# A two-layer decoder on one core: shift and scale sums by transposes with VectorE's part two blocks later, constants among the first weight blocks, and the up-projection's relu and square on ScalarE

## The chip, the cores and the metric

The kernel runs on one core of a Trainium2 chip. The metric is the time of one execution on the device in microseconds (us); a median over several runs is given. Five engines work side by side, each in the order of its own queue: PE (TensorE, matrix products into PSUM, with PEld its weight loads), DVE (VectorE), ACT (ScalarE), POOL (GpSimd) and SP (SyncE, which here issues all the DMA transfers). An engine waits only where an instruction needs something that another engine or a transfer has not delivered.

## The reference, cut to what matters

Two decoder layers on 256 rows of 2048 columns. Each layer takes six vectors of 2048 from one condition vector c (shift, scale and gate, for attention and for the MLP), and uses shift and scale to turn x into the input h of a projection.

```python
c_act = jax.nn.silu(c)
for l in range(DEPTH):
    mod = c_act @ w_ada[l] + b_ada[l]                 # w_ada[l]: 2048 x 12288
    sh_a, sc_a, g_a, sh_m, sc_m, g_m = jnp.split(mod[:, None, :], 6, axis=-1)
    h = x * (1.0 + sc_a) + sh_a
    y = _mixer(h, ...)                                # input projection, attention, output projection
    x = _layernorm(ALPHA * x + (1.0 + g_a) * y, ln1_g[l], ln1_b[l])
    h = x * (1.0 + sc_m) + sh_m
    y = jnp.square(jax.nn.relu(h @ w_up[l])) @ w_down[l]
    x = _layernorm(ALPHA * x + (1.0 + g_m) * y, ln2_g[l], ln2_b[l])
```

All is float32. Each product is formed from a high and a low part in a shorter format (`hi*hi + hi*lo + lo*hi`), so a weight block is split once, and every output needs three products.

## The kernel before, in words

**Blocks.** Weights come in blocks of 128 partitions x 1024 numbers (512 KB). A block is loaded into `raw` by SP (L139; 7 buffers), copied into a high part `wh` by ACT (L133), and DVE subtracts to get the low part `wl` (L134; 3 buffers each for `wh` and `wl`). PE then runs the products of the block (L290 to L292, L316 to L319, or L897 and L899 in the up-projection). The function `block` counts blocks; between blocks it does other pieces of work that are queued in lists.

**The condition vectors.** They stream through the same `raw` buffers (`rawa`, L155 and L183) among the weight blocks, at a rate per block (`side_rate`). In `ada_T` DVE multiplies 16 such blocks by one number per partition each and adds them up in `acc` (L145 for the first, L147 for the other 15; `acc` has one buffer). That leaves 128 partitions x 2 x 512 partial sums, which have to be added over the partitions and laid out with the column number on the partition. `finish` does it: PE multiplies each 128 columns of `acc` by a column of ones (L163, eight products of one column each, which the profile shows as 16 instructions), into one PSUM bank, and DVE adds the bias (L167, two instructions) to get four columns of two vectors in `modT`. There are 16 such finishes, four for each pair of vectors. A finish is put into `pending`, and `settle` runs it at the next block or when its result is wanted. The gate vectors go through `ada_G`, with a finish of their own.

**The start.** Layer 0's input projection runs in four passes over a quarter of the depth each (`first_pass`), since h of a quarter needs the shift and scale of that quarter only. Before the first pass come 16 blocks `rawa`, a finish, and `make_h`: PE transposes x (L460), ACT applies scale and shift (L473), DVE splits h into `hT` (L475, L476). The constants (masks, the tables sin and cos, the transposed norm parameters, lambda) are set up by `constants()` between those 16 blocks. Before each later pass, again, a finish and a `make_h` have to be through.

**The up-projection.** Four PSUM tiles are filled per 512 columns. In `up_out` ACT copies one half of each out (L914), DVE adds the other half (L915) and forms max(t,0)*t (L916), ACT copies the high part of the result into `Hs` (L923), DVE subtracts for the low part (L924). For the first eight sets of layer 0, which run in two halves (`part` is given), ACT forms relu and square instead (L919, L920).

**The order.** Each engine's instructions are put in order when the program is built, by a scheduler that goes by priorities (the order of the code) and by estimated durations; tiles wait for a free buffer of their pool. PSUM has four buffers for products (`mm`) and four for all else (`bank`).

## Time and profile before

| | before |
|---|---|
| time, median of 3 runs | 2384.29 us (2381.55 to 2387.99) |
| the profiled execution: its time | 2385.05 us |
| the profiled execution: its span | 2383.3 us |
| busy PE / DVE / ACT | 2300.8 / 1798.7 / 1106.1 us |
| DMA, mean rate | 260 GB/s |

The span is what the trace covers; the execution took 1.75 us more. Busy time is the sum over an engine's instructions without overlap. PE's busy time contains whatever its pipeline leaves between two products, so it is read by the starts of successive instructions as well. In a row of the list of instructions the first number is the start, the second the time, and a bracket says how long the engine was idle before it and what ended that.

### The profile page before, as it was taken

The numbers are of one execution on the slowest core, as the hardware profiler recorded it, in microseconds if no ns is written. First come the engines' busy times: TensorE is split into PE (matmuls) and PEld (weight loads), VectorE is DVE, ScalarE is ACT, GpSimd is POOL, SyncE is SP. The second block draws the span as 40 slices with busy tenths as digits, with TensorE's granted clock in tenths as the row PEclk, the third lists the DMA queues.
The fourth block names the chain that finished last, engine by engine and source line by source line (L and its number), as shares of the span: only waits on it lengthen the run. The fifth ranks groups of instructions, "written<-read, shape, count | busy, mean of one in ns | idle before, by whom it ended". The sixth has DMA issues, their size and how long they took to land.

```text
span 2383.3 us, 33425 instructions
## 1 busy us (share of the span) xinstructions
PE 2300.8 (97%) x12572; PEld 1977.8 (83%) x12572; DVE 1798.7 (75%) x2355; ACT 1106.1 (46%) x1589; POOL 36.9 (2%) x60
## 2 busy tenths in 40 slices
PE   4999999899999999999999999999999999999998
PEld 3887798799989788888877778977888888888886
DVE  7788988878888678879877876667685666665667
ACT  3543675344546344344444564544444443543442
POOL 0000010000000000000000000000000000000000
PEclk9999999999999999999999999999999999999999
DMA  9999688888998888888858977764687777756653
GB/s 313 341 321 314 203 265 302 315 295 308 321 326 306 281 284 307 303 281 301 290 175 290 311 225 242 234 214 168 218 267 247 230 236 247 230 191 192 187 190 124
DMA packets 309891, 619.39 MB, mean 260 GB/s; under 512 B 24200, under 2 KB 25048, under 8 KB 309728
## 3 DMA queue, kind: packets, MB, share of 16 engines
q1 hardware_dynamic: 309728, 617.25, 77.0%
q8 instruction: 98, 1.61, 0.3%
q14 instruction: 65, 0.53, 0.1%
HBM read 615.07 MB, written 2.10 MB: 259 GB/s over the span
## 4 chain that ended last, share of the span: by engine, by line
PE 81%; DVE 8%; DMA 6%; issue 3%; ACT 2%; POOL 0%; DVEq 0%; SPq 0%; ACTq 0%; POOLq 0%
PE mm L291 13%; PE mm L292 13%; PE mm L290 13%; PE mm L897 7%; PE bank L897 7%; PE mm L319 5%; PE mm L318 5%; PE mm L316 5%; DMA rawa<-in_w_ada_dram 5%; PE mm L899 4%; PE bank L899 4%; DVE wl L134 3%; DVE acc L147 2%; PE bank L163 1%; DMA raw<-in_w_in_dram 1%
## 5 line engine op out<-in xcount | busy, mean ns | idle before, releaser
L133 ACT CAST wh<-raw 128x1024 fp32r<-128x1024 f32 x752 | 788.9, 1052 | 958.5 <-PE mm L292 493.0
L134 DVE TENSOR_TENSOR wl<-raw,wh 128x1024 fp32r<-128x1024 f32 x752 | 913.5, 1221 | 345.6 <-ACT wh L133 341.8
L147 DVE SCALAR_TENSOR_TENSOR acc<-rawa,cact,acc 128x1024 f32<-128x1024 f32 x368 | 471.1, 1280 | 138.4 <-DMA rawa<-in_w_ada_dram 136.7
L291 PE MATMUL mm<-wl,Hs 128*128 128x512 f32 x992 | 386.7, 390 | 3.2 <-DVE wl L134 3.2
L290 PE MATMUL mm<-wh,Hs 128*128 128x512 f32 x992 | 386.2, 389 | 0.0
L292 PE MATMUL mm<-wh,Hs 128*128 128x512 f32 x992 | 386.1, 389 | 0.0
L319 PE MATMUL mm<-hT,wl 128*128 128x256 f32 x1024 | 289.4, 285 | 4.8 <-DVE wl L134 4.8
L316 PE MATMUL mm<-hT,wh 128*128 128x256 f32 x1024 | 291.1, 286 | 1.5 <-DVE hT L475 1.1
L318 PE MATMUL mm<-hT,wh 128*128 128x256 f32 x1024 | 290.3, 284 | 0.8 <-DVE hT L476 0.8
L897 PE MATMUL mm<-hT,wh 128*128 128x512 f32 x768 | 288.0, 398 | 0.1
L897 PE MATMUL bank<-hT,wh 128*128 128x512 f32 x768 | 287.0, 396 | 0.0
L291 PEld LDWEIGHTS mm<-wl,Hs 128*128 128x128 f32 x992 | 186.2, 188 | 43.8 <-DVE wl L134 5.3
L290 PEld LDWEIGHTS mm<-wh,Hs 128*128 128x128 f32 x992 | 186.2, 188 | 38.8
L292 PEld LDWEIGHTS mm<-wh,Hs 128*128 128x128 f32 x992 | 186.2, 188 | 38.4
L899 PE MATMUL mm<-hT,wl 128*128 128x256 f32 x768 | 215.6, 281 | 1.0 <-DVE wl L134 1.0
L899 PE MATMUL bank<-hT,wl 128*128 128x256 f32 x768 | 215.2, 280 | 0.0
L291 PE MATMUL mm<-wl,hT 128*128 128x512 f32 x512 | 202.6, 396 | 2.0 <-DVE wl L134 1.8
L290 PE MATMUL mm<-wh,hT 128*128 128x512 f32 x512 | 199.8, 400 | 3.0 <-DVE hT L475 3.0
L319 PEld LDWEIGHTS mm<-hT,wl 128*128 128x128 f32 x1024 | 196.6, 193 | 6.4 <-DVE wl L134 6.2
L292 PE MATMUL mm<-wh,hT 128*128 128x512 f32 x512 | 200.8, 393 | 0.6 <-DVE hT L476 0.6
L316 PEld LDWEIGHTS mm<-hT,wh 128*128 128x128 f32 x1024 | 197.5, 193 | 3.1 <-DVE hT L475 1.4
L318 PEld LDWEIGHTS mm<-hT,wh 128*128 128x128 f32 x1024 | 197.6, 193 | 1.5 <-DVE hT L476 1.3
(249 smaller groups left out, 2653.7 us busy)
## 6 DMA issues: line engine op xcount, KB each, us to landing
rawa<-in_w_ada_dram SPq DMA_DIRECT2D x384, 512.0 KB, 5.3
raw<-in_w_up_dram SPq DMA_DIRECT2D x256, 512.0 KB, 4.6
raw<-in_w_down_dram SPq DMA_DIRECT2D x256, 512.0 KB, 5.2
raw<-in_w_in_dram SPq DMA_DIRECT2D x192, 512.0 KB, 5.4
raw<-in_w_o_dram SPq DMA_DIRECT2D x64, 512.0 KB, 5.3
gb<-in_ln_g_dram SPq DMA_DIRECT2D x12, 256.0 KB, 6.2
bb<-in_ln_b_dram SPq DMA_DIRECT2D x12, 256.0 KB, 6.9
xacc<-in_x_dram SPq DMA_DIRECT2D x8, 256.0 KB, 6.5
```

Source lines behind the costliest of these rows:

```text
L133: nc.scalar.copy(wh, raw)
L134: nc.vector.tensor_sub(wl, raw, wh.bitcast(F32))
L147: nc.vector.scalar_tensor_tensor(acc, raw, k, acc, ALU.mult, ALU.add)
L163: nc.tensor.matmul(ps[:, f:f + 1], lhsT=acc[:, f // 4, (f % 4) * P:(f % 4 + 1) * P], rhs=ones[:, 0:1], start=True, stop=True)
L290: nc.tensor.matmul(o, lhsT=hi, rhs=wh, start=start, stop=False)
L291: nc.tensor.matmul(o, lhsT=hi, rhs=wl, start=False, stop=False)
L292: nc.tensor.matmul(o, lhsT=lo, rhs=wh, start=False, stop=stop)
L316: nc.tensor.matmul(o, lhsT=wh[:, j, cs], rhs=hT[:, kt, 0, :], start=first and kt == kt0 and f % 2 == 0, stop=False)
L318: nc.tensor.matmul(o, lhsT=wh[:, j, cs], rhs=hT[:, kt, 1, :], start=False, stop=False)
L319: nc.tensor.matmul(o, lhsT=wl[:, j, cs], rhs=hT[:, kt, 0, :], start=False, stop=last and kt == kt1 - 1 and f % 2 == 1)
L897: nc.tensor.matmul(pu[f], lhsT=wh[:, j, cs], rhs=hT[:, kt].rearrange("p a s -> p (a s)"), start=kt == kt0, stop=False)
L899: nc.tensor.matmul(pu[f][:, 0:S], lhsT=wl[:, j, cs], rhs=hT[:, kt, 0, :], start=False, stop=kt == kt1 - 1)
```

## The change

The diff does three things. (1) The finish of a shift and scale sum: eight transposes of 128x128 into two PSUM banks in place of eight products with a column of ones, then, on DVE, one sum over the free axis for each bank (`reduce_sum`) and the addition of the bias. `finish` is now a generator: its PE part runs as before, its DVE part two blocks later (`LATER`), unless the result is wanted before. The four finishes of the first passes and whatever else is asked for by key run through at once. A gate's finish keeps its parts together and counts as ready two blocks later. (2) The start: the loads of three `rawa` blocks come ahead of x, the masks on POOL and the bias come next, and the rest of the constants is handed out one piece per block inside the first pass. (3) In `up_out` relu and square are two ACT instructions for all sets, where DVE had one.

```diff
+LATER = 2
@@
-    ones = const.tile([P, P], F32, name="ones")
-    nc.vector.memset(ones, 1.0)
+    one = const.tile([P, 1], F32, name="one")
+    nc.vector.memset(one, 1.0)
     ones_r = const.tile([P, P], F32R, name="ones_r")
-    nc.vector.tensor_copy(ones_r, ones)
+    nc.vector.memset(ones_r.bitcast(F32), 1.0)
@@
         def finish():
-            ps = bank()
-            for f in range(8):
-                nc.tensor.matmul(ps[:, f:f + 1], lhsT=acc[:, f // 4, (f % 4) * P:(f % 4 + 1) * P],
-                                 rhs=ones[:, 0:1], start=True, stop=True)
+            pss = []
             for i in range(2):
+                ps = bank()
+                for f in range(4):
+                    nc.tensor.transpose(ps[:, f * P:(f + 1) * P], acc[:, i, f * P:(f + 1) * P], ident)
+                pss.append(ps)
+            yield
+            for i, ps in enumerate(pss):
+                red = sm.tile([P, 4], F32, tag="red", name="red")
+                nc.vector.reduce_sum(red, ps.rearrange("p (f k) -> p f k", f=4), axis=mybir.AxisListType.X)
                 s0 = (vec + i) * KT + kt0
-                nc.vector.scalar_tensor_tensor(modT[l, vec + i][:, kt0:kt0 + 4], ps[:, 4 * i:4 * i + 4], float(i),
+                nc.vector.scalar_tensor_tensor(modT[l, vec + i][:, kt0:kt0 + 4], red, float(i),
                                                badaT[l][:, s0:s0 + 4], ALU.add, ALU.add)
 
-        pending[(l, vec, kt0)] = finish
+        pending[(l, vec, kt0)] = [0, finish()]
@@
     def settle(*keys):
-        for k in keys or list(pending):
-            if k in pending:
-                pending.pop(k)()
-                ready.add(k)
+        for k in list(keys or pending):
+            while k in pending and (keys or pending[k][0] <= count[0]):
+                if next(pending[k][1], keys) is keys:
+                    del pending[k]
+                    ready.add(k)
+                elif not keys:
+                    pending[k][0] = count[0] + LATER
+                    break
@@
-                    nc.vector.scalar_tensor_tensor(t2, t2, 0.0, t2, ALU.max, ALU.mult)
                 else:
                     nc.vector.tensor_add(t2, pu[f2 // 2], part[:, f2:f2 + 2, :])
-                    nc.scalar.activation(t2, t2, AF.Relu)
-                    nc.scalar.activation(t2, t2, AF.Square)
+                nc.scalar.activation(t2, t2, AF.Relu)
+                nc.scalar.activation(t2, t2, AF.Square)
@@
         if i == 0:
-            side.extend([x_rows(a, b)] + want_mod(0, 0, [a]))
-            side_pop()
+            side.extend(want_mod(0, 0, [a]))
+            for _ in range(3):
+                side_pop()
+            for _ in x_rows(a, b):
+                pass
+            bias_T(0)
+            masks()
             for k2 in range(a, b, 2):
                 turned[k2] = turn(k2)
-            for _ in constants():
-                side_pop()
         side_flush()
@@
+        if i == 0:
+            rest = constants()
+            for _ in range(12):
+                later.append(lambda: next(rest, None))
```

**Order at the start.** SP's issues from the first instruction of the program on, before (`crow` is c, `xacc` x, `r_...` and the small names are constants):

```order
L101 DMA crow<-in_c_dram 16x128
L1005 DMA xacc<-in_x_dram 128x512 x2
L384 DMA pos_i<-in_positions_dram 128x2x1
L119 DMA r_153<-in_b_ada_dram 96x128
L155 DMA rawa<-in_w_ada_dram 128x2x512
L419 DMA r_193<-in_ln_g_dram 32x128
L155 DMA rawa<-in_w_ada_dram 128x2x512
L419 DMA r_193<-in_ln_b_dram 32x128
L155 DMA rawa<-in_w_ada_dram 128x2x512
```

and in the changed program (the same queue, the same place):

```order
L102 DMA crow<-in_c_dram 16x128
L156 DMA rawa<-in_w_ada_dram 128x2x512 x3
L1015 DMA xacc<-in_x_dram 128x512 x2
L120 DMA r_119<-in_b_ada_dram 96x128
L156 DMA rawa<-in_w_ada_dram 128x2x512 x13
L140 DMA raw<-in_w_in_dram 128x2x512
```

The first `rawa` moves ahead of four other issues, and eleven small transfers are gone from among the 16. On ACT, before, the first instructions after the program's entry are these (the table for Sin, then sin of the angles, then the table for Silu and `cact`, by which all `rawa` are multiplied):

```order
L412 ACT_TABLE_LOAD
L412 ACTIVATE sinT<-ang 128x16
L107 ACT_TABLE_LOAD
L107 ACTIVATE cact<-bank 128x16
L413 ACTIVATE cosT<-ang 128x16
```

and in the changed program:

```order
L108 ACT_TABLE_LOAD
L108 ACTIVATE cact<-bank 128x16
L1019 ACTIVATE xacc<-xacc 128x512 x2
L134 CAST wh<-raw 128x1024 x2
L484 ACTIVATE h_222<-bank,mod_0_105,mod_1_106 128x256 x2
```

`cact` no longer stands behind the sine.

**Order at the first layer norm.** DVE's instructions at the change from attention to MLP in layer 0, before (`mv`, `ve`, `rs` are a row's statistics, L501 normalizes, L167 is the finish):

```order
L494 TENSOR_SCALAR ve<-mv 128x1
L488 BN_STATS stats<-xacc 128x6
L501 TENSOR_SCALAR xacc<-xacc,mv,rs 128x512 x4
L492 BN_AGGR mv<-stats 128x2
L167 SCALAR_TENSOR_TENSOR mod_3_1877<-bank,badaT_157 128x4
L494 TENSOR_SCALAR ve<-mv 128x1
L167 SCALAR_TENSOR_TENSOR mod_4_1878<-bank,badaT_157 128x4
L134 TENSOR_TENSOR wl<-raw,wh 128x1024
L501 TENSOR_SCALAR xacc<-xacc,mv,rs 128x512 x2
```

and in the changed program:

```order
L503 BN_AGGR mv<-stats 128x2
L148 SCALAR_TENSOR_TENSOR acc<-rawa,cact,acc 128x1024
L505 TENSOR_SCALAR ve<-mv 128x1
L503 BN_AGGR mv<-stats 128x2
L135 TENSOR_TENSOR wl<-raw,wh 128x1024
L512 TENSOR_SCALAR xacc<-xacc,mv,rs 128x512 x4
L505 TENSOR_SCALAR ve<-mv 128x1
L135 TENSOR_TENSOR wl<-raw,wh 128x1024
L512 TENSOR_SCALAR xacc<-xacc,mv,rs 128x512 x2
L171 TENSOR_REDUCE red<-bank 128x4 x2
```

The finish's DVE part stands behind the second row's statistics and its normalization; an accumulation (L148) has moved in ahead of the first row's.

**Order after a set of the up-projection.** ACT's instructions at the end of one full set, before:

```order
L914 COPY t_8769<-mm 128x256 x2
L914 COPY t_8777<-bank 128x256
L133 CAST wh<-raw 128x1024
L914 COPY t_8777<-bank 128x256
L923 CAST Hs<-t_8769 128x2x256
L133 CAST wh<-raw 128x1024
L923 CAST Hs<-t_8777 128x2x256
L133 CAST wh<-raw 128x1024 x6
```

and in the changed program:

```order
L925 COPY t_8821<-mm 128x256 x2
L925 COPY t_8830<-bank 128x256
L134 CAST wh<-raw 128x1024
L925 COPY t_8830<-bank 128x256
L929 ACTIVATE t_8821<-t_8821 128x512
L930 ACTIVATE t_8821<-t_8821 128x512
L929 ACTIVATE t_8830<-t_8830 128x512
L933 CAST Hs<-t_8821 128x2x256
L930 ACTIVATE t_8830<-t_8830 128x512
L134 CAST wh<-raw 128x1024
L933 CAST Hs<-t_8830 128x2x256
L134 CAST wh<-raw 128x1024 x6
```

Between the first and the second copy of a weight block there now stand five instructions where there were two. On PE the order of the weight products outside attention is nearly the same in both programs; where L163 stood eight times, L166 (the transpose) stands eight times. In the first passes the transposes of x have moved: ahead of the third pass all eight stand directly before the first product that needs them, where six had stood 34 products earlier.

## Rows read from the trace of the kernel before

**Rows 1.** The page's first part: busy time and share of each engine.
```profile
PE 2300.8 (97%) x12572; PEld 1977.8 (83%) x12572; DVE 1798.7 (75%) x2355; ACT 1106.1 (46%) x1589; POOL 36.9 (2%) x60
```
**Rows 2.** Stretches of 60 us: busy time of each engine, granted clock, DMA share, GB/s.
```profile
0.00:60.00 60.00, 27.95 (x110) 22.76 (x111) 42.32 (x73) 18.72 (x27) 4.08 (x28) 1.00 0.91 313
60.00:120.00 60.00, 58.64 (x359) 52.00 (x359) 47.22 (x46) 31.93 (x41) 0.00 (x0) 1.00 0.96 342
720.00:780.00 60.00, 60.00 (x444) 57.31 (x443) 50.79 (x51) 36.42 (x48) 0.00 (x0) 1.00 0.87 295
2340.00:2384.00 44.00, 32.19 (x143) 26.31 (x141) 30.66 (x42) 8.87 (x9) 1.83 (x2) 0.90 0.27 97
```
**Rows 3.** PE's waits over the span: total us, times, longest.
```profile
PE bank L121 <- DVE dots L436: 11.6, 1, 11.6
...
PE mm L291 <- DVE wl L134: 6.4, 9, 1.4
```
**Rows 4.** List of instructions, the start: start us, us, engine, line.
```profile
2.63 0.26 PE L105 MATMUL bank<-ident,crow 16*128 16x16 f32 x1 [2.63 <-DMA crow<-in_c_dram]
...
3.18 0.43 SPq L155 DMA_DIRECT2D rawa<-in_w_ada_dram  x1
...
4.92 1.76 PE L460 MATMUL bank<-ident,xacc 128*128 128x128 f32 x7 [0.24 <-DMA xacc<-in_x_dram]
...
9.15 1.28 ACT L107 ACT_TABLE_LOAD   x1
...
10.66 0.75 DVE L145 TENSOR_SCALAR acc<-rawa,cact 128x1024 f32<-128x1024 f32 x1 [1.78 <-ACT cact L107]
...
21.84 0.28 DVE L436 TENSOR_REDUCE dots<-ta 128x2 f32<-128x128 f32 x1
...
28.31 5.25 DVE L147 SCALAR_TENSOR_TENSOR acc<-rawa,cact,acc 128x1024 f32<-128x1024 f32 x4 [0.25 <-DVE acc L147]
...
33.71 3.54 PE L163 MATMUL bank<-ones,acc 128*128 128x1 f32 x16 [8.06 <-DVE acc L147]
...
39.09 0.79 PE L290 MATMUL mm<-wh,hT 128*128 128x512 f32 x1 [1.84 <-DVE hT L475]
```
**Rows 5.** One stretch of 3 us near the start, columns as in group 2.
```profile
27.00:30.00 3.00, 0.00 (x0) 0.00 (x0) 2.71 (x3) 0.00 (x0) 0.00 (x0) 1.00 1.06 388
```
**Rows 6.** List of instructions: a finish, and eight transposes, each with what follows.
```profile
249.25 1.03 PE L576 MATMUL bank<-ident,early 128*128 128x128 f32 x8
...
250.04 0.48 PE L290 MATMUL mm<-wh,hT 128*128 128x512 f32 x1
...
812.74 1.84 PE L163 MATMUL bank<-ones,acc 128*128 128x1 f32 x16
...
814.44 0.49 PE L290 MATMUL mm<-wh,Hs 128*128 128x512 f32 x1
```
**Rows 7.** Line L167: what its engine waited for, us and times.
```profile
  PE bank L163: 29.6, 14
```
**Rows 8.** List of instructions at the first layer norm.
```profile
474.08 3.41 PE L163 MATMUL bank<-ones,acc 128*128 128x1 f32 x16
...
477.53 0.16 DVE L167 SCALAR_TENSOR_TENSOR mod<-bank,badaT 128x4 f32<-128x4 f32 x1 [2.38 <-PE bank L163]
...
480.00 1.33 PE L460 MATMUL bank<-ident,xacc 128*128 128x128 f32 x5 [1.59 <-DVE xacc L501]
```
**Rows 9.** List of instructions where the fourth pass begins.
```profile
219.69 0.50 PE L290 MATMUL mm<-wh,hT 128*128 128x512 f32 x1 [1.14 <-DVE hT L475]
```
**Rows 10.** Lines L916 and L919: ns min/median/max, first and last start; one block's copies.
```profile
L916 DVE SCALAR_TENSOR_TENSOR t<-t x48: 680/682/693, 881.3 to 2288.4; 128x512 f32<-128x512 f32 x48
...
L919 ACT ACTIVATE t<-t x16: 614/624/635, 596.8 to 769.8; 128x512 f32<-128x512 f32 x16
...
875.13 1.05 ACT L133 CAST wh<-raw 128x1024 fp32r<-128x1024 f32 x1 [1.77 <-PE bank L897]
876.21 1.22 DVE L134 TENSOR_TENSOR wl<-raw,wh 128x1024 fp32r<-128x1024 f32 x1 [1.59 <-ACT wh L133]
```

More of the change, by code (lines that the diff above doesn't have):

```diff
@@ L196, in finish @@
                     nc.tensor.matmul(ps, lhsT=ones_r, rhs=lo[:, 0, qs], start=False, stop=True)
-                    nc.scalar.activation(g[:, qs], ps, AF.Identity, bias=ones[:, 0:1])
-            pending[(l, vec, "gate", half)] = finish
+                    nc.scalar.activation(g[:, qs], ps, AF.Identity, bias=one)
+                yield
+            pending[(l, vec, "gate", half)] = [0, finish()]
             yield 1
@@ L244, in side_flush @@
             side_pop()
-        settle()
+        settle(*pending)
     def gate_part(key, half):
@@ L354, in decoder, with masks @@
     lnT = const.tile([P, 4, DEPTH, KT], F32, name="lnT")
-    def constants():
+    def masks():
         nc.gpsimd.memset(mhalf, -0.5)
@@ L380, in constants @@
                                 base=-2 * NF, pattern=[[0, 1]], channel_multiplier=1)
+    def constants():
         pos_i = const.tile([P, NT], I32, name="pos_i")
         nc.sync.dma_start(pos_i, positions[0].rearrange("(t p) -> p t", p=P))
-        yield
-        bias_T(0)
         yield
```

## The prediction

> **What bounds the kernel now.** I read the busy times first, then the same in stretches of 60 us, PE's waits, the start, and last each place that the change touches. PE is busy for 2300.8 of 2383.3 us [rows 1], 82.5 us idle. Of these 60 - 27.95 = 32.1 lie in the first stretch and 44 - 32.19 = 11.8 in the last; in between whole stretches have no idle time at all [rows 2]. Behind the start the waits are small: the largest that recurs, for a weight block's low part, comes to 6.4 us in nine times [rows 3]. So work taken off PE comes off the span wherever DMA and DVE can follow, and they are close behind: in the stretch from 60 us on DMA is at 0.96 and DVE at 47.22 of 60 [rows 2]. Work taken off DVE or ACT shows only where PE waits for it. The profiled execution took 2385.05 us, 1.75 over its span and 0.76 over the median of the runs; I sum against 2385.05 and take the 0.76 off at the end.
>
> **The start.** Before, the first product of a weight block begins at 39.09, and 16 accumulations on DVE end at 28.31 + 5.25 = 33.56 [rows 4]. They begin at 10.66, held by `cact`: the sine stands ahead of it on ACT and waits for the positions, and a second table load of 1.28 follows at 9.15 [rows 4]. Without the sine ahead of it `cact` follows its transpose (2.63 + 0.26) at about 3. The first `rawa` is issued at 3.18, behind four issues that go away; at 0.43 to 0.47 each it comes near 1.3. x, issued just there, was ready for PE at 4.92 [rows 4], so the first `rawa` lands near 4.6. From there the 16 blocks are paced by transfer: 524 KB at 388 GB/s [rows 5] is 1.35 us, a little over DVE's 1.31 (5.25/4). The last lands at 4.6 + 15 x 1.35 + 1.35 for x = 26.2, and DVE is through at 27.5, 6 earlier. Behind it, before: 39.09 - 33.56 = 5.5. After: eight transposes at 0.25 (seven took 1.76 here [rows 4]) make 2.0, against 3.54. Then DVE reduces bank one, subtracts a weight block (1.22), reduces bank two; with a reduce at 0.68 (below), 2 x 0.56 of ACT and 0.43 of DVE for h, PE starts near 33.1. I take **-5.5**. Bounds: -3.5 if early transfers run at the 313 GB/s of the whole stretch [rows 2] and the constants' absence buys little; -7.5 if DVE sets the pace and the second subtraction falls elsewhere.
>
> The constants don't vanish: 34 small DVE instructions, 12 transfers, two of ACT and two PE transposes now lie in the first pass, one step a block. At most 0.28 each [rows 4], 34 make 9.5 us, in a stretch where DVE idles 60 - 47.22 = 12.8 [rows 2]. The cover is thin: DMA has 0.04 x 60 = 2.4 us free there. I charge **+1.0**, bounds 0 and +6.
>
> **The finishes on PE.** Start to start, sixteen L163 instructions take 814.44 - 812.74 = 1.70 us; eight transposes of 128x128 take 250.04 - 249.25 = 0.79 [rows 6]. Two of the 16 finishes are counted elsewhere (start, first norm); 14 x 0.91 = **-12.7**. It is off PE itself, in a queue that otherwise hardly changes. Bounds: -14 and, where a finish's gain turns into a wait for DMA or DVE, -6.
>
> The Trainium skill, "TensorE: Matmul & The Clock Gate", Part 4: PE-mode transpose, speaks against this: a 128x128 transpose is said to take about 275 ns in a kernel. By that eight take 2.2 us, more than the products they replace, and the 14 finishes would cost about +7. The rows have the same length for one (1.03 for the eight with 0.79 between first and next start, [rows 6]) but the next starts 0.1 us later: they overlap, and I go by the starts.
>
> **DVE's part.** Bias additions waited 29.6 us for PE in 14 finishes [rows 7], in front of low parts of weight blocks. Two blocks later PE is through and that wait is gone. New are 32 reductions of 512 numbers per partition out of PSUM. The trace has none: 0.28 for 128 numbers [rows 4] is one end, 1.28 for 1024 with three operands the other (a quarter of the 5.25 in [rows 4]); I take 0.68, DVE's time for 512 numbers of L916 [rows 10]: 22 us, less than the waits. PE waited little behind them, so this is 0, bounds -3 and +2. Each finish now holds two of four banks for two blocks; before the up-projection's next set the other two are its own, so I see no wait there.
>
> **Later passes.** Their finishes run through at once, as before. At the fourth pass, before, all eight transposes of x stand directly ahead of the first product that needs h, and PE waits 1.14 [rows 9]. In the changed order the third pass looks so too, where six had stood 34 products earlier, and the second pass has its transposes in one piece as well: one such wait and a third of another, **+1.5**, bounds 0 and +4.
>
> **First layer norm.** The finish ran at the slow pace of idle PE, 3.41; DVE waited 2.38 for it with the second row's statistics queued behind, and PE then 1.59 for the normalized row [rows 8]. Now the reduction stands behind. But an accumulation of 1.28 stands ahead of the first row's statistics. PE saves about 3.41 - 2.0; I take **-1.5**, bounds -3.3 and +1. The other three norms keep their order.
>
> **Up-projection.** DVE loses 48 x 0.68 = 33 us, ACT gains 96 x 0.62 = 60 [rows 10]. Between two copies of weight blocks ACT now has 4 x 0.62 + 0.37 = 2.85, where a block lasts 1.05 + 1.77 = 2.82 [rows 10]; that copy slips by 2.85 + 1.05 - 2.82 = 1.1. With three buffers PE has two more blocks, 5.64, when a copy is released, and copy and subtraction take 2.3: slack 3.3. So 0. The same chain already runs for 16 pieces from 596.8 to 769.8 [rows 10], and PE has no idle time in the stretch from 720 on [rows 2]. Bounds -3 (DVE freed in layer 0) and +2.
>
> The Trainium skill, "ScalarE: Activation LUTs", Rules for kernel authors, says the opposite of this edit: relu and multiplication belong on VectorE. In fp32 the rows are near equal for one instruction (0.62 and 0.68) but ACT needs two. It would matter only if ACT set the pace, as in the last rival.
>
> **Sum.** -5.5 + 1.0 - 12.7 + 1.5 - 1.5 = -17.2; 2385.05 - 17.2 - 0.76 = 2367.1, so **2367 us**. Below 2377 it is faster by over 0.3%, about what a measurement of this kernel can tell from no change; above 2391.5 slower by as much.
>
> **Rivals.** (a) *DMA paces.* DMA share is 0.87 to 0.96 in the stretches of layer 0 [rows 2], and the earlier start asks for the same bytes sooner. Then only the lower start gain, -3.5, and four finishes in stretches where PE never idles, -3.6, survive: 2377. Against: PE waits only 6.4 us for the commonest low part [rows 3]. (b) *Transposes don't overlap where they stand among weight products*: at the start's 1.76/7 = 0.25 each [rows 4] eight take 2.0, 0.3 more than the products; 14 x 0.3 = +4.2 in place of -12.7 gives 2384, no change. Against: the starts, among weight products too [rows 6]. [...] (c) *Two banks held*: in layer 1's attention three finishes hold half the banks for two blocks (5.6 us); PE stands for them, +17, and the time is about 2384. For: the heads use the same four; against: PE's order there hardly changes, so no early use is forced. (d) *Slower: ACT delays the weights.* If a copy's real slack is under its slip, each of 24 full sets stops PE. Slack gone entirely, all four pieces of 0.62 count: 24 x 2.5 = +60, 2427; half, 2397. It decides once a copy comes more than 3.3 late. Against: the stretch at 720 [rows 2].
>
> **Chances.** Forecast 0.71 (its own range 2357 to 2376), (a) 0.16, a third of it faster, (b) 0.03, (c) 0.04, (d) 0.06. Faster 0.76, same 0.18, slower 0.06. The range runs from start, constants, finishes, passes and norm all at their good ends (-24.8) and a part of DVE's relief, -27 or 2357, to (a) and a little above, 2380.
>
> **What would show it.** The first weight product near 33.5; 16 accumulations ended near 27.5; eight transposes in 0.8 between starts; the reduction near 0.7; no bracket over 1 us for PE behind the bank's reduction; PE without idle time in the up-projection. It is wrong if PE's idle time grows by about what the finishes save, if the first pass has waits for low parts, or if the first product still starts past 36.

## The result and the profile after

| | before | after |
|---|---|---|
| median of 5 runs, us | 2382.98 (2378.37 to 2387.99) | 2369.63 (2367.95 to 2374.72) |
| profiled execution, us (span) | 2385.05 (2383.3) | 2369.32 (2367.6) |

The ratio is 0.9948, 95% interval 0.9931 to 0.9965: faster, by 8 to 16 us. Forecast was 2367, with a range of 2357 to 2380.

First the page's busy times of the changed kernel, answering to [rows 1]. PE has 128 instructions fewer and is busy 19.5 us less. ACT is busy 49 us more and DVE only 9 less, since DVE's 32 reductions (21.5 us) are new.

```profile
PE 2281.3 (96%) x12444; PEld 1959.6 (83%) x12444; DVE 1790.1 (76%) x2339; ACT 1155.3 (49%) x1684; POOL 35.1 (1%) x60
```

The most useful view of this case cuts each span at the first product of a weight block, because PE behind it is nearly gapless. Two stretches of the kernel before (columns: from:to, length, busy time and instructions of PE, PEld, DVE, ACT, POOL, granted clock, DMA share, GB/s):

```profile
0.00:39.09 39.09, 7.04 (x29) 5.79 (x29) 26.55 (x58) 8.18 (x14) 4.08 (x28) 1.00 0.93 323
39.09:2383.30 2344.21, 2293.74 (x12544) 1971.99 (x12544) 1772.20 (x2298) 1097.95 (x1576) 32.86 (x32) 0.99 0.77 259
```

The same two of the changed kernel:

```profile
0.00:37.14 37.14, 4.32 (x18) 3.48 (x18) 24.65 (x27) 6.24 (x10) 4.08 (x28) 1.00 0.97 342
37.14:2367.60 2330.46, 2277.00 (x12426) 1956.17 (x12426) 1765.43 (x2313) 1149.01 (x1675) 31.01 (x32) 0.99 0.78 260
```

The span fell by 15.7: the first product comes 1.95 earlier, PE is busy 16.74 less behind it, and idle 53.46 instead of 50.47, 2.99 more. Read in stretches of 5 us, the granted clock is 1.0 nearly everywhere and between 0.5 (1.2 GHz) and 1.0 in a few. One minus the clock, times the stretch and summed, says how much the lower level took away: 17.8 us before, 14.3 after. So of the 16.74 some 3.5 are clock, and 13.2 are work that PE no longer does. The column can't be read for the first few microseconds, though: the trace's first record of the clock comes at 43.8 us before and at 41.7 after, and where there is none the column says 1.00. The products ahead of that record run at the slower pace, as two rows of the changed kernel show; this costs both kernels alike some 2.3 us (an estimate: half of the time from the first product to the first record) and is in neither sum.

```profile
41.15 0.63 PE L302 MATMUL mm<-wh,hT 128*128 128x512 f32 x1
...
42.12 0.39 PE L302 MATMUL mm<-wh,hT 128*128 128x512 f32 x1
```

The start of the changed kernel, in the order of time, against [rows 4]. `cact` is ready at 3.04 and the first accumulation starts at 5.02. Then DVE stands for 5.88 us at the copy of the bias rows, and only from 11.84 do fifteen accumulations run back to back, to 31.61.

```profile
2.86 0.18 ACT L108 ACTIVATE cact<-bank 128x16 f32<-128x16 f32 x1 [0.78 <-PE bank L106]
...
5.02 0.75 DVE L146 TENSOR_SCALAR acc<-rawa,cact 128x1024 f32<-128x1024 f32 x1 [3.93 <-DMA rawa<-in_w_ada_dram]
...
11.20 0.42 PE L122 MATMUL bank<-ident,r 96*128 96x96 f32 x1 [8.38 <-DMA r<-in_b_ada_dram]
11.66 0.26 DVE L124 COPY badaT<-bank 128x96 f32<-128x96 f32 x1 [5.88 <-PE bank L122]
11.84 19.77 DVE L148 SCALAR_TENSOR_TENSOR acc<-rawa,cact,acc 128x1024 f32<-128x1024 f32 x15
...
31.75 1.94 PE L166 MATMUL bank<-ident,acc 128*128 128x128 f32 x8 [18.42 <-DVE acc L148]
32.87 0.69 DVE L171 TENSOR_REDUCE red<-bank 128x4 f32<-128x512 f32 x1 [1.27 <-PE bank L166]
...
37.14 0.79 PE L302 MATMUL mm<-wh,hT 128*128 128x512 f32 x1 [3.45 <-DVE hT L486]
```

A finish of the changed kernel among weight products, against [rows 6]: the next product starts 0.80 after the first of the eight transposes, where sixteen instructions had taken 1.70.

```profile
426.58 1.03 PE L166 MATMUL bank<-ident,acc 128*128 128x128 f32 x8
427.38 0.47 PE L302 MATMUL mm<-wh,MXd 128*128 128x512 f32 x1
```

The new reduction, and what DVE and PE waited for (total us, times, longest). DVE's wait for a finish fell from 29.6 in 14 [rows 7] to 10.0 in nine.

```profile
L171 DVE TENSOR_REDUCE red<-bank x32: 673/684/692, 32.9 to 1586.2; 128x4 f32<-128x512 f32 x32
...
DVE red L171 <- PE bank L166: 10.0, 9, 2.4
...
PE bank L471 <- DVE xacc L512: 15.0, 4, 6.9
...
PE mm L303 <- DVE wl L135: 6.4, 8, 1.7
```

### The profile page after: what moved, and what is told of

The parts are those of the page before. It is cut to its first block, busy times and chain, and to the rows that moved or that the text cites. A ratio compares the mean times of both kernels' runs of the same rounds, so it can differ in the third digit from the quotient of the medians.

```text
span 2367.6 us, 33293 instructions
## 1 busy us (share of the span) xinstructions
PE 2281.3 (96%) x12444; PEld 1959.6 (83%) x12444; DVE 1790.1 (76%) x2339; ACT 1155.3 (49%) x1684; POOL 35.1 (1%) x60
## 3 DMA queue, kind: packets, MB, share of 16 engines
q8 instruction: 97, 1.59, 0.3%
## 4 chain that ended last, share of the span: by engine, by line
PE 76%; DVE 9%; DMA 9%; issue 3%; ACT 2%; POOL 0%; SPq 0%; DVEq 0%; ACTq 0%; POOLq 0%
PE mm L303 13%; PE mm L302 13%; PE mm L304 13%; PE mm L908 7%; PE bank L908 7%; DMA rawa<-in_w_ada_dram 5%; PE mm L331 4%; PE mm L330 4%; PE mm L328 4%; PE mm L910 4%; PE bank L910 4%; DVE wl L135 4%; DVE acc L148 2%; DMA raw<-in_w_in_dram 1%; ACT wh L134 1%
## 5 line engine op out<-in xcount | busy, mean ns | idle before, releaser
L148 DVE SCALAR_TENSOR_TENSOR acc<-rawa,cact,acc 128x1024 f32<-128x1024 f32 x368 | 471.0, 1280 | 137.8 <-DMA rawa<-in_w_ada_dram 136.5
```

Of the source, the lines that this page charges most:

```text
L148: nc.vector.scalar_tensor_tensor(acc, raw, k, acc, ALU.mult, ALU.add)
```

## The experiments

Each ratio is to the kernel before, measured in the same rounds, with its 95% interval. The table makes the cut of above for every kernel, from its one profile. "Work" is PE's busy time behind the first product less the time lost at the lower clock; a loss can fall where PE is idle too, and in all but the kernel with the doubled transposes the slow pace ahead of the first clock record is not counted, so it is good to a microsecond or two.

| kernel | ratio | first product | lost at lower clock | work | idle behind it |
|---|---|---|---|---|---|
| before | 1 | 39.09 | 17.8 | 2275.9 | 50.5 |
| up-projection alone | 1.0000 | 40.56 | 14.8 | 2278.2 | 48.8 |
| start alone | 0.9998 | 37.00 | 19.3 | 2275.7 | 51.9 |
| products, sum later | 0.9998 | 40.11 | 19.7 | 2274.3 | 47.5 |
| transposes, sum at once | 1.0016 | 39.33 | 24.5 | 2264.5 | 59.7 |
| finishes alone | 0.9978 | 41.67 | 18.2 | 2262.1 | 56.8 |
| finishes + up-projection | 0.9978 | 39.80 | 21.7 | 2261.0 | 56.5 |
| finishes + start | 0.9962 | 37.11 | 17.7 | 2263.6 | 53.3 |
| the change | 0.9948 | 37.14 | 14.3 | 2262.7 | 53.5 |
| bias rows first | 0.9954 | 35.90 | 15.7 | 2263.2 | 54.4 |
| sum one block later | 0.9962 | 37.09 | 17.9 | 2263.3 | 52.7 |
| sum four blocks later | 0.9967 | 36.49 | 21.7 | 2262.4 | 54.8 |
| transposes twice | 1.0031 | 37.81 | 26.9 | 2272.9 | 55.0 |
| wait at the norm filled | 0.9943 | 36.88 | 9.5 | 2272.3 | 51.1 |

### One part at a time

*Finishes alone*: the kernel before with the new finish and `settle`.

```diff
-                nc.tensor.matmul(ps[:, f:f + 1], lhsT=acc[:, f // 4, (f % 4) * P:(f % 4 + 1) * P],
-                                 rhs=ones[:, 0:1], start=True, stop=True)
...
+                    nc.tensor.transpose(ps[:, f * P:(f + 1) * P], acc[:, i, f * P:(f + 1) * P], ident)
...
+            yield
...
-        pending[(l, vec, kt0)] = finish
+        pending[(l, vec, kt0)] = [0, finish()]
```

> The kernel before with the finish alone changed (transposes, DVE's sum two blocks later); start and up-projection as before. Theory 1 (time comes off PE: each of 14 finishes gives 0.9 us between starts, and the first layer norm some us): 9 to 15 us faster than before, spread over the span, about 4 us of it in the MLP of layer 0 with its four finishes. Theory 2 (time comes from DVE: waits and multiplies that are gone): 2 to 6 us, none of it in stretches where PE never idles. Theory 3 (where DMA and DVE pace, a finish gives nothing): 0 up to 470 us, 4 at the first norm, the rest in the MLP of layer 0; 7 to 10 us in all.

Measured 2378.85 against 2384.98, ratio 0.9978 (0.9966 to 0.9989).

*Up-projection alone*: the kernel before without DVE's relu and square.

```diff
-                    nc.vector.scalar_tensor_tensor(t2, t2, 0.0, t2, ALU.max, ALU.mult)
...
+                nc.scalar.activation(t2, t2, AF.Relu)
+                nc.scalar.activation(t2, t2, AF.Square)
```

> The kernel before with relu and square of the up-projection on ACT alone. Theory 1: no change (within 2 us), since PE has no idle time there and ACT has slack. Theory 2: 3 to 5 us faster, all of it in the MLP of layer 0 (780 to 1140 us), where PE had about 4 us of idle time behind low parts of weight blocks; nothing in layer 1's MLP. Rival (ACT delays the weight copies): slower, PE idle in both MLPs.

Measured 2384.08, ratio 1.0000 (0.9991 to 1.0009): nothing, either way.

*Start alone*: the kernel before with the new order of the start and the constants in the first pass.

```diff
-            side.extend([x_rows(a, b)] + want_mod(0, 0, [a]))
+            side.extend(want_mod(0, 0, [a]))
+            for _ in range(3):
+                side_pop()
...
+            rest = constants()
+            for _ in range(12):
+                later.append(lambda: next(rest, None))
```

> The kernel before with the start alone changed (rawa ahead of x, constants into the first pass); finishes and up-projection as before. If an earlier start carries through: first weight product 1 to 2 us earlier than 39.09 and the span 1 to 2 us shorter. If the first passes are paced by DMA and DVE, or the constants cost there what they gave before: no change (within 1 us), the gain lost before 250 us.

Measured 2385.27, ratio 0.9998 (0.9986 to 1.0009). The first product comes at 37.00, 2.09 earlier, and the time does not follow: in the profile 1.5 us of idle time and 1.5 of lower clock stand against it. The lead is gone before the fourth pass is through, as the second theory had it: ACT copies the 71st weight block at 251.4 us in this kernel and at 249.5 in the one before. In between PE waits 3.8 us for low parts of weight blocks, for which the kernel before hardly waits there.

So the finishes are the part that pays by itself, 5 us, and they pay some 8 less than PE's work fell by (13.8 in the table): idle time behind the first product rose by 6.3, and the first product came 2.6 later. None of the three theories for them fits whole: the size is that of the second, but the MLP of layer 0 gains 5.6 us (506.7 to 501.1), where PE had hardly been idle.

### What in the finish pays

Two kernels split the finish: the products kept and only DVE's part moved, and the transposes with DVE's part directly behind them.

```diff
             for f in range(8):
                 nc.tensor.matmul(ps[:, f:f + 1], lhsT=acc[:, f // 4, (f % 4) * P:(f % 4 + 1) * P],
                                  rhs=ones[:, 0:1], start=True, stop=True)
+            yield
```

> The kernel before, with its sixteen one-column products as they were, but VectorE's bias addition two weight blocks after them. TensorE's time for a finish stays at 1.70 us; VectorE's 14 waits for TensorE (29.6 us in the kernel before) should fall to near nothing. Theory one (the gain of the finishes is the time taken off TensorE): no gain, ratio 0.999 to 1.001, MLP of layer 0 at 506 to 507 us. Theory two (the gain comes from VectorE being released from its wait): the gain of the finishes alone, ratio 0.998, that MLP at 501 us.

Measured 2381.96 against 2382.42, ratio 0.9998 (0.9988 to 1.0007). The expectation on the wait failed. It only moved: eight times DVE still waits at the bias addition, and six times at the next set's first accumulation, which writes what the products read. 28.7 us in sum, as before:

```profile
DVE mod L169 <- PE bank L164: 16.8, 8, 3.7
DVE acc L146 <- PE bank L164: 11.9, 6, 2.4
```

So this run does not test what the release of DVE alone is worth; it shows that being later alone gives nothing.

```diff
-            yield
             for i, ps in enumerate(pss):
                 red = sm.tile([P, 4], F32, tag="red", name="red")
                 nc.vector.reduce_sum(red, ps.rearrange("p (f k) -> p f k", f=4), axis=mybir.AxisListType.X)
```

> The kernel before with the transposes in place of the products, and VectorE's sum directly behind them instead of two blocks later. TensorE's time for a finish falls as in the change; VectorE waits for it 14 times again (near 29 us in sum), and has two reductions of 0.68 more there. Theory one (TensorE's time): the gain of the finishes alone, ratio 0.998, MLP of layer 0 at 501 us. Theory two (VectorE's release): none of it, ratio 1.000 to 1.002, that MLP at 506 to 509 us.

Measured 2387.53, ratio 1.0016 (1.0006 to 1.0025): slower than before, though PE's work fell by 11 us. DVE waits for the transposes no more than in the finishes alone (9.2 us in eight against 10.4 in nine), where near 29 were expected. The profile has 9.3 us more idle time and 6.7 more at the lower clock, and the MLP of layer 0 takes 510.5 us, 3.8 more than before. One such place in that MLP: an accumulation waits on DVE for its transfer, three low parts follow, and PE stands. Behind it the granted clock is 0.83 in both stretches of 5 us from 800 to 810; in the kernel before no stretch of this MLP is below 1.00.

```profile
799.63 1.28 DVE L147 SCALAR_TENSOR_TENSOR acc<-rawa,cact,acc 128x1024 f32<-128x1024 f32 x1 [2.70 <-DMA rawa<-in_w_ada_dram]
800.83 3.49 DVE L134 TENSOR_TENSOR wl<-raw,wh 128x1024 fp32r<-128x1024 f32 x3
...
802.10 0.50 PE L295 MATMUL mm<-wl,Hs 128*128 128x512 f32 x1 [2.01 <-DVE wl L134]
```

Theory one of both expectations, that TensorE's time is all there is to it, falls with this run. Theory two has the ratio right and not the reason: DVE's wait is as short here as in the finishes alone, so it is the transposes that shorten the wait, and what the delay gives is something else. Neither edit gains anything without the other. One difference is not told apart: in this run a gate's finish also counts as ready at once, in the finishes alone two blocks later. That the sum at once puts the accumulations behind their transfers' rhythm is argued from places like this one and not shown.

*Twice the transposes*, in the changed kernel:

```diff
-                for f in range(4):
+                for f in [0, 1, 2, 3] * 2:
```

> The changed kernel with each of the eight transposes of a finish issued twice into the same place, which adds 8 x 0.1 = 0.8 us to TensorE at each of some 14 finishes, about 11 us, and nothing to VectorE, ScalarE or the transfers. Theory one (after the first product TensorE is nearly without gaps, so its time is the kernel's): 2370 + 9 to 12 = 2379 to 2382 us, ratio to the kernel before 0.999 to 1.000. Theory two (the time is set by VectorE or by transfers, and TensorE's share only fills idle time): 2370 to 2374 us, ratio 0.995 to 0.997.

Measured 2389.95 against 2383.08, ratio 1.0031 (1.0018 to 1.0044), 20 us over the change where 9 to 12 were expected. Sixteen transposes take 1.66 from start to start, 0.86 more than eight:

```profile
433.50 1.91 PE L166 MATMUL bank<-ident,acc 128*128 128x128 f32 x16
435.16 0.47 PE L302 MATMUL mm<-wh,MXd 128*128 128x512 f32 x1
```

Work rose by 10.2, and idle time by 1.6: what PE must do more does come out as time. The rest of this profile's rise is the clock, 26.9 lost instead of 14.3. Here the record begins at 34.9 us, and the slow products at 38 to 42 count as lost clock; in the changed kernel the same products, with their 2.3 us, count as work. By one measure for both, work rose by some 12.5 us, near fifteen times 0.86, and the clock took some 10. The lower clock is not in this profile alone: over the span it is 0.988 to 0.992 in the seven runs and 0.991 to 0.995 in the five of the change. That the added transposes bring the lower clock about is not shown: of the doubled kernel's other ten stretches at the lower level only one lies beside any, at 479 to 482 (the norm).

*How much later.*

```diff
-LATER = 2
+LATER = 1
```

> The changed kernel with VectorE's part of a finish one weight block after the transposes instead of two. If one block is enough cover (the transposes end within a microsecond and a block lasts 2.8 us or more): the time of the change, ratio 0.994 to 0.996, and VectorE's wait for the transposes stays near 10 us. If two are needed: VectorE's wait grows toward the 29 us of the kernel before and the ratio to 0.997 to 0.999.

Measured 2374.38, ratio 0.9962 (0.9947 to 0.9976); DVE waits 10.0 us in nine, as with two.

```diff
-LATER = 2
+LATER = 4
```

> The changed kernel with VectorE's part of a finish four weight blocks after the transposes. If two banks held longer cost nothing: ratio 0.994 to 0.996. If the banks are what other work waits for: TensorE's waits for a bank grow and the ratio goes to 0.997 or more.

Measured 2375.59, ratio 0.9967 (0.9954 to 0.9980); DVE waits 10.1 in nine, and PE's list of waits has none for a reduction. Both intervals overlap that of the change. One block is cover enough, and no wait in the trace is for banks held over four blocks; a loss of a few microseconds by them the ratio could not tell.

### Two parts together

The change without its new start:

```diff
-            for _ in range(3):
-                side_pop()
...
+            side.extend([x_rows(a, b)] + want_mod(0, 0, [a]))
```

> The change without its new start: transposes with VectorE's part two blocks later, and the up-projection's square on ScalarE. If the parts simply add: ratio 0.998 and MLP of layer 0 near 501 us. If the up-projection's move gives something only once the finishes are off VectorE's path: that MLP near 498 us as in the whole change, and the ratio near 0.997. The first passes should stay near 253 us as with the finishes alone if the new start is what the whole change gains there.

Measured 2377.66, ratio 0.9978 (0.9969 to 0.9987), first passes 251.1 and MLP of layer 0 500.1 us. "First passes" is the time from the span's start to the copy of the 71st weight block on ACT: 249.5 before, 253.5 with the finishes alone, 245.2 in the change.

The change with DVE's old share of the up-projection:

```diff
+                    nc.vector.scalar_tensor_tensor(t2, t2, 0.0, t2, ALU.max, ALU.mult)
...
-                nc.scalar.activation(t2, t2, AF.Relu)
-                nc.scalar.activation(t2, t2, AF.Square)
+                    nc.scalar.activation(t2, t2, AF.Relu)
+                    nc.scalar.activation(t2, t2, AF.Square)
```

> The change with VectorE's old share of the up-projection: transposes with VectorE's part two blocks later, and the new start. If the parts simply add: ratio 0.998. If finishes and start help each other in the first passes: those near 245 us, ratio near 0.996, MLP of layer 0 at 501 us. If the whole change's 498 us in that MLP comes from where its blocks fall and not from the up-projection's square: 498 us here too, ratio 0.995.

Measured 2374.65, ratio 0.9962 (0.9949 to 0.9974), first passes 245.7 and that MLP 499.6 us. Cut where ACT copies the same blocks, the MLP of layer 0 in the kernel before and in the changed one:

```profile
602.46:1109.12 506.66, 503.70 (x2746) 436.18 (x2745) 413.71 (x435) 232.34 (x274) 1.91 (x2) 1.00 0.88 301
```

```profile
594.05:1092.43 498.38, 498.05 (x2714) 432.96 (x2713) 411.48 (x432) 245.63 (x297) 1.91 (x2) 1.00 0.89 306
```

So over half of the span's 15.7 us are gained here; 4.3 are there by the end of the first passes, 4.1 come between the two, and none behind this MLP (below). Of its 8.3 us the finishes bring 5.6 alone (501.1) and 7.0 with the new start. The square on ScalarE brings nothing without the finishes (507.3), and whether it brings 1 us with them (501.1 to 500.1, 499.6 to 498.4) is not shown: the four other kernels with all three parts (bias rows first, sum one and four blocks later, wait at the norm filled) take 499.1 to 501.6 us for it.

The start is different: alone nothing can be measured, but beside the finishes the ratio goes from 0.9978, twice, to 0.9943 to 0.9967 in the six kernels that have both. Part of it is in the table: with the old start the first product comes anywhere from 39.1 to 41.7 us (six kernels, mean 40.1), and in their traces DVE waits at the start for transfers that land at other times in each; with the new one, where DVE runs back to back from the bias copy on, at 36.5 to 37.1 (six, leaving out the bias rows first and the doubled transposes, mean 37.0). The remainder is idle time, 51 to 55 us with both and 57 with the finishes alone, and lower clock. Most of it lies in the first passes: behind the first product the two kernels with the finishes and the old start have 6.6 us of idle time there and 1.7 to 3.4 lost to the clock, the change and the kernel above 4.3 and none. I have no cause for it that a run shows.

### The start's missing four microseconds

```diff
+            bias_T(0)
             for _ in range(3):
                 side_pop()
             for _ in x_rows(a, b):
                 pass
-            bias_T(0)
```

> The changed kernel with the bias of the condition vectors loaded directly behind c, ahead of the first three rawa (there its copy stood second on DVE and held the accumulations 5.9 us). If that copy is what kept the start from its forecast: DVE's 16 accumulations end near 27.5 to 28.5 in place of 31.6, first weight product near 33 to 34 in place of 37.1, and the span 3 to 4 us under the changed kernel if it carries through. If the first passes are paced by DMA: the same first product, but the gain is gone by the fourth pass and the span is the same within 1 us. If the accumulations are paced by DVE or DMA anyway: first product after 36.

Measured 2372.52, ratio 0.9954 (0.9938 to 0.9969): no better than the change. The bias copy no longer blocks, and the first product comes at 35.90, only 1.24 earlier, since now the fourth block of weights is what comes late:

```profile
3.53 0.26 DVE L124 COPY badaT<-bank 128x96 f32<-128x96 f32 x1 [2.44 <-PE bank L122]
...
8.62 1.28 DVE L148 SCALAR_TENSOR_TENSOR acc<-rawa,cact,acc 128x1024 f32<-128x1024 f32 x1 [0.21 <-DMA rawa<-in_w_ada_dram]
12.88 17.55 DVE L148 SCALAR_TENSOR_TENSOR acc<-rawa,cact,acc 128x1024 f32<-128x1024 f32 x13 [2.97 <-DMA rawa<-in_w_ada_dram]
31.63 0.69 DVE L171 TENSOR_REDUCE red<-bank 128x4 f32<-128x512 f32 x1 [1.21 <-PE bank L166]
```

### The first layer norm's clock

At the first norm PE waits 6.86 us, the clock falls in that wait, and PE goes on at the lower level. This kernel fills the wait with products that nobody reads.

```diff
+            if key == (0, 2) and ch == 3 and t == 0:
+                ps = bank()
+                for _ in range(8):
+                    nc.tensor.matmul(ps, lhsT=ident, rhs=tmp, start=True, stop=True)
```

> The changed kernel with eight extra products of 128x512 float values (ident with the gated sum's first tile, into a bank that nobody reads) placed where TensorE waits 6.9 us for the first layer norm of layer 0. Theory one (the clock falls there because TensorE stands still, and the 10.2 us at the lower granted clock that follow the wait cost about 5 us): the granted clock stays near 1.00 from 465 to 480 us, and the kernel gains 2 to 5 us over the change, ratio 0.993. Theory two (the layer norm is paced by VectorE there, and TensorE's clock is hidden behind it): the clock may rise, and the time stays, ratio 0.994 to 0.996. Theory three (the products end later than the wait and delay the norm's transposes): 1 to 4 us lost, ratio 0.995 to 0.997.

Measured 2371.07 against 2383.55, ratio 0.9943 (0.9924 to 0.9962): the change's time. Stretches of 10 us, first of the changed kernel, then of this one:

```profile
460.00:470.00 10.00, 5.59 (x25) 4.31 (x23) 9.93 (x16) 4.03 (x4) 0.00 (x0) 0.92 1.05 389
470.00:480.00 10.00, 6.45 (x33) 5.93 (x34) 8.72 (x22) 1.93 (x4) 3.03 (x2) 0.57 0.58 188
```

```profile
460.00:470.00 10.00, 9.95 (x32) 5.63 (x31) 9.53 (x15) 3.14 (x3) 1.56 (x1) 1.00 0.95 344
470.00:480.00 10.00, 7.53 (x53) 6.06 (x52) 9.45 (x22) 3.68 (x8) 1.47 (x2) 1.00 0.45 147
```

The clock stays at its upper level, so it had fallen because PE stood still; but the weight blocks behind are reached no sooner. From the copy of the up-projection's first block, at the norm, to that of its eleventh it is 36.8 us in the changed kernel and 36.7 in this one. DVE is busy for 18.7 and 19.0 of the 20 us: it sets the pace, as theory two had it, and the lower clock there costs next to nothing.

## Why the prediction was right, and where it was not

In the terms of the cut, for the profiled executions (the clock's -3.5 was in no step):

| | forecast | profile |
|---|---|---|
| start, to the first product | -5.5 | -1.95 |
| finishes on PE | -12.7 | -13.2 |
| idle behind it: constants, passes, norm, DVE | +1.0 | +3.0 |
| lower clock | 0 | -3.5 |
| sum | -17.2 | -15.7 |

The sum came within 1.5 us of the forecast, and partly by luck: the start gave 3.5 us less than forecast, and the clock, which was in no step, gave 3.5 back. What the clock takes differs from profile to profile, 9.5 to 26.9 us in the table above, so no run credits its 3.5 to the change.

**The finishes on PE** were right, and for the reason given: 0.80 between starts, work of 2261 to 2265 us in every kernel with transposes (the doubled ones apart, and 7.1 of filler taken off), of 2274 to 2278 in every kernel with products. The step counted 14; fifteen stand behind the first product, the norm's among them. The Trainium skill, "TensorE: Matmul & The Clock Gate", Part 4: PE-mode transpose, gives some 275 ns for one; that eight take eight times as long, 2.2 us, is an estimate from that figure. The trace agrees with the length of one (273 ns), not with the estimate: eight take 0.80 from start to start. So rival (b) is out.

**DVE's part** was right in its sizes, 0.684 for the reduction (0.68 taken) and no wait for a bank, and too small in its weight. I costed it at 0 between -3 and +2. Taking the delay away turns the finishes' -5 us into +4, from 0.9978 to 1.0016. I had treated the move behind two blocks as a way to save DVE a wait, and that is not what it does: the products with the sum two blocks later leave DVE waiting 28.7 us, and the transposes with the sum at once 9.2. What it saves shows in the idle time and clock elsewhere, and the way there stays open.

**The start** was the failed step: "the 16 blocks are paced by transfer: 524 KB at 388 GB/s", last accumulation at 27.5. It ended at 31.61, and from 11.84 on DVE itself set the pace, 1.32 us a block. The first accumulation came as forecast (5.02 for 4.6), but 388 was read at 27 to 30 us [rows 5] and set against the first ten. There the stretch from 6 to 9 us shows 251, and one microsecond of it 139:

```profile
3.00:6.00 3.00, 0.00 (x0) 0.00 (x0) 0.75 (x1) 0.04 (x1) 1.71 (x14) 1.00 1.01 350
6.00:9.00 3.00, 0.00 (x0) 0.00 (x0) 0.00 (x0) 0.00 (x0) 0.00 (x0) 1.00 0.95 251
8.00:9.00 1.00, 0.00 (x0) 0.00 (x0) 0.00 (x0) 0.00 (x0) 0.00 (x0) 1.00 0.80 139
9.00:12.00 3.00, 0.80 (x4) 0.80 (x5) 0.34 (x2) 0.00 (x0) 0.00 (x0) 1.00 0.96 334
12.00:15.00 3.00, 1.33 (x7) 0.93 (x5) 2.93 (x3) 1.15 (x2) 0.00 (x0) 1.00 1.05 401
```

It is a dip and not a slow beginning: from 5 to 6 us the rate is 377 already. What makes it no run shows. The bias rows, too, I had counted only among the issues that leave the queue ahead of the first block, and DVE's wait for them was in no term. By the bias-first run that wait is 1.2 of the 4.1 us; the rest stands in that run as DVE's waits for transfers. Behind the accumulations the 5.53 to the first product (31.61 to 37.14) is what was forecast, 5.6. The sign of being wrong, "the first product still starts past 36", was therefore met, and the step is wrong, though the sum was not.

**Later passes, norm, constants.** The third pass waits as said, for the same 1.14 as the fourth:

```profile
157.87 0.50 PE L302 MATMUL mm<-wh,hT 128*128 128x512 f32 x1 [1.14 <-DVE hT L486]
...
216.35 0.50 PE L302 MATMUL mm<-wh,hT 128*128 128x512 f32 x1 [1.14 <-DVE hT L486]
```

But another wait for `hT`, of 0.6, went away, and in the first passes PE is idle for 4.3 us where it had been for 3.8: +0.5 in place of the +2.5 charged for the passes and the constants. Of the +3.0, 1.2 more are added up to the MLP of layer 0 (at the norm, `xacc`), that MLP takes 2.6 off, and 3.9 are added behind it (see the rivals). At the first norm the transposes take 1.91 where products had taken 3.41 [rows 8], as forecast (2.0), and PE's second bracket is 1.10 in place of 1.59:

```profile
472.45 0.66 PE L471 MATMUL bank<-ident,xacc 128*128 128x128 f32 x2 [6.86 <-DVE xacc L512]
472.90 1.91 PE L166 MATMUL bank<-ident,acc 128*128 128x128 f32 x8
475.91 3.06 PE L471 MATMUL bank<-ident,xacc 128*128 128x128 f32 x14 [1.10 <-DVE xacc L512]
```

But the first bracket grew: the accumulation ahead of the statistics, which I had allowed for, makes it 6.9 where the longest had been 5.2. The stretch around the norm is nonetheless 4.0 shorter over ten weight blocks (2.3 ahead of it, 6.3 behind).

**Up-projection**: 0 was right, the ratio of that edit alone is 1.0000 (0.9991 to 1.0009), and the MLP of layer 0 has PE idle for 0.33 of 498.38 us, so rival (d) is out. The Trainium skill's rule in "ScalarE: Activation LUTs", Rules for kernel authors, that relu and multiplication belong on VectorE, made no difference to the time here, since neither engine set PE's pace in the up-projection.

**The rivals.** (a) is seen in part, and where it had not been looked for. Behind the MLP of layer 0 the change gains nothing, although four of the finishes lie there, 3.6 us off PE by their starts; idle time rises by 3.9. First the kernel before, then the changed one:

```profile
1109.12:2383.30 1274.18, 1244.78 (x6477) 1056.20 (x6475) 876.61 (x1158) 585.09 (x827) 16.51 (x17) 0.99 0.69 225
```

```profile
1092.43:2367.60 1275.17, 1241.89 (x6445) 1052.13 (x6443) 861.71 (x1130) 622.53 (x899) 14.28 (x17) 0.99 0.69 225
```

What grows are PE's waits for low parts, from 5.3 us to 9.8; in these stretches, before and after:

```profile
PE mm L291 <- DVE wl L134: 2.7, 4, 1.2
PE mm L319 <- DVE wl L134: 2.6, 2, 1.4
```

```profile
PE mm L331 <- DVE wl L135: 5.1, 4, 2.0
PE mm L303 <- DVE wl L135: 4.7, 7, 1.5
```

The longest of them stands behind an accumulation that DVE had to wait for:

```profile
1444.98 1.28 DVE L148 SCALAR_TENSOR_TENSOR acc<-rawa,cact,acc 128x1024 f32<-128x1024 f32 x1 [4.47 <-DMA rawa<-in_w_ada_dram]
...
1447.46 0.39 PE L331 MATMUL mm<-hT,wl 128*128 128x256 f32 x1 [2.02 <-DVE wl L135]
```

Five such places make 6.0 us there, three made 3.7 before, so about half of that growth stands behind transfers. At the norm and in the first passes it is DVE that PE waits for. The forecast had held against (a) that the largest recurring wait is the 6.4 us for low parts [rows 3]. It was not: PE waited longer at the norms, as this row of the kernel before shows, and for low parts 12.2 us over all lines of products.

```profile
PE bank L460 <- DVE xacc L501: 13.8, 4, 5.2
```

(c) is out: the four-block run has no wait for a bank that a reduction holds, and its ratio, 0.9954 to 0.9980, lies below the 1.000 of that rival.

## What to carry to other kernels

When one engine is nearly gapless behind a first event, cut the span there and account for three numbers: that event's time, the engine's busy time less what the lower clock took, and its idle time; single parts of a change are then seen even where their times aren't. Cut it once more by stage, since a gain can be whole in one and eaten up in the next. A rate read from the steady middle of a load did not hold for its first ten microseconds here. Taking work off the busy engine paid here only with the reader's part moved out of the way as well: try the two edits apart before crediting either.

## What was not expected of the hardware

- Early transfers: 251 GB/s from 6 to 9 us at a DMA share of 0.95, with a dip to 139 from 8 to 9; 401 from 12 to 15. With the bias rows first the fourth block of the condition weights was usable only at 12.9.
- The granted clock falls at the norm with PE standing still (0.57 over 470 to 480) and stays at 1.00 when products fill that wait; 128x512 products of plain float32 take two instructions, sixteen in 7.13 us, 0.45 each.
- Some 12.5 us of added transposes made the kernel 20 us slower; in the one profile some 10 us more went to the lower clock, for which no run shows the cause.
